# Hybrid chunk-causal layer: weights around the per-layer-input weights requested four tiles ahead, the first two up units' sums on VectorE, the second norm's rows two products later

## The chip, the cores and the metric

One core of one Trainium2 chip runs the whole layer. The metric is the device time of one execution in microseconds; the kernel before was run three times (median 2042.41, from 2042.25 to 2044.58), and once more with the hardware profiler on.

## What is computed

The reference is one layer for two groups of requests: 1024 rows of a prompt and 32 rows of a sample step, 1056 rows of 1024 numbers in all, in float32. Cut to what the change touches:

```python
mix = jax.nn.sigmoid(ga) * (ya @ w_br_a) + jax.nn.sigmoid(gb) * (yb @ w_br_b)
x = x + _rms_norm(mix @ w_out, g_post_mix)
hf = _rms_norm(x, g_pre_ffn)
a, u = jnp.split(hf @ w_up, 2, axis=-1)
...
ffn = (jax.nn.gelu(ac, approximate=True) * u) @ w_down
x = x + _rms_norm(ffn, g_post_ffn)
x = x + (pe @ w_ple) * jax.nn.sigmoid(x @ w_ple_gate)
```

Here `ac` is the causal convolution of `a` over three rows, `pe` the per-layer input (256 numbers a row), `w_up` is 1024 by 5632, `w_out` 1024 by 1024, `w_ple` 256 by 1024.

## The kernel before

**Products.** Everything is kept transposed: 128 features on the partitions, rows along the free dimension. A float32 operand is split into a high and a low part (`hi` is the rounded copy, `lo = x - hi`), and a product is three products of TensorE: high by high, high by low, low by high (lines 193 to 195 in `product`, 1536 to 1538 in the up stage). ScalarE makes the high part and VectorE the low one.

**Weights.** `load_raw` asks SyncE's queue for a raw tile of 512 KB (tag `wr`, two buffers). `load_next` makes its two parts (tag `wb`, eight buffers, so four weights at a time): the high part in line 174 on ScalarE, the low part in line 177 on VectorE; the raw buffer is free again after the low part. `next_w(ahead=2)` goes on with `load_next` until the weight asked for and `ahead` more are there. The list `plan` gives the order of the weights. At the place of the change it holds `w_out` columns 0 to 4, then the two tiles of `w_ple`, then `w_out` columns 5 to 7. Below, c0 to c7 are those eight column blocks of `w_out`, and ple0 and ple1 the two tiles of `w_ple`. The parts of ple0 and ple1 stay in their `wb` buffers until the last `ple_product`.

**The stretch that the change touches.** `w_out` is applied twice: first for rows 0 to 527 (`p` = 0, groups 0 and 1 of 264 rows), then for rows 528 to 1055 (`p` = 1, groups 2 and 3). A block is 24 products for each of the two groups. Beside the second pass, the first half is normed and prepared: `pair_norm` sums squares over the features with TensorE (`sums88`, line 1271, one-column products), takes the inverse root on VectorE (`rsqrt`, lines 204 to 210, twelve small instructions in a chain) and spreads it over the partitions with TensorE (`norm_rows`, line 294), from where ScalarE copies it to `rbT` (line 296). `x1_part` forms the new x (VectorE, lines 1294 and 1295), stores it by GpSimd's queue and scales it (ScalarE, line 1298); `x1_squares` squares it; `build_ops` makes the seven right operands of a Strassen-Winograd scheme (`op`, casts in line 1325, low parts in line 1326, sums and differences in lines 1329 to 1337). After c7 come `pair_norm(1, 0.25 / D)`, four `ple_product` (groups 0 to 3, each of eight blocks of six products, copied by ScalarE in line 1360 and stored by GpSimd's queue) and, between them, `x1_part(2)`, `x1_part(3)` and `build_ops(1)`.

**Up units.** Then 22 up units follow, each 128 columns of both halves of `w_up`. `unit_raw` loads the two raw tiles (even units in the `wr` buffers), `unit_parts` makes seven left operands: four sums (lines 1389 to 1391 and 1396, on GpSimd before) and seven pairs of parts (`wt`, lines 1383 and 1384). `up_unit` runs seven steps; in a step, `mults` makes 12 products for each half `p`, into one of three PSUM tiles X, Y, Z, and `after` moves the result on. Unit 0 does the two halves one after the other, and in a different order for the second half (`early`). `last_ops` squares x of rows 528 to 1055 (line 1509) and sums the squares (24 one-column products for each group, the sums of groups 2 and 3) beside unit 0's first half; the norm that they give, `pair_norm(1, 1.0 / D, x1_t[0])`, is called in unit 0's second half. Its result `rbT` is needed by `after(2)` (line 1551), which scales X into `ab`.

**What sets the order.** The program text gives each instruction its priority; a scheduler then orders each engine's instructions by priority and by the times that it expects, and gives out buffers. Each engine runs its own list strictly in that order, and an instruction that waits holds up all behind it. Each DMA queue is in order too.

Of the kernel before, what the change touches and what calls it, by code (L numbers as in the profile page):

```python
# [14 lines left out]
ALU = mybir.AluOpType  # L15
# [3 lines left out]
D = 1024  # L19
# [11 lines left out]
H = 264  # L31
# [3 lines left out]
T88 = ((0, 88), (88, 88), (176, 88))  # L35
# [24 lines left out]
def layer_kernel(  # L60
# [17 lines left out]
    def nm(s):  # L78
        n_names[0] += 1
        return f"{s}_{n_names[0]}"  # L80
# [5 lines left out]
    V, S, G, E = nc.vector, nc.scalar, nc.gpsimd, nc.tensor  # L86
# [95 lines left out]
    def next_w(ahead=2):  # L182
        while len(ready) < min(limit[0], used[0] + 1 + ahead):
            load_next()
        used[0] += 1
        return ready[used[0] - 1]
# [44 lines left out]
    def tr_bank():  # L231
        return bank(pp, "tr", 2)
# [56 lines left out]
    def norm_rows(rs, tiles, out):  # L289

        n = sum(m_ for _, m_ in tiles)
        t = tr_bank()
        for i, (c, m_) in enumerate(tiles):
            E.matmul(t[:, c:c + m_], rs[:m_, i:i + 1].to_broadcast([m_, P]), ident[:m_, :m_],  # L294
                     start=True, stop=True)
        S.copy(out, t[:, :n])
# [7 lines left out]
    with right("ap") as ap:  # L304
# [198 lines left out]
        with tc.tile_pool(name="np", bufs=1, side="right", reuse_waits="tile") as np_:  # L503
# [103 lines left out]
            xt, rs, rb = ([], [], []), [], []  # L607
            for n in range(6):
# [3 lines left out]
                if n == 2:  # L612
                    rows = vector_rows()
# [73 lines left out]
    for j in range(4):  # L687
# [3 lines left out]
        for k in (0, 2):  # L691
# [3 lines left out]
                            op=ALU.subtract)  # L695
# [84 lines left out]
    with right("bp") as bp:  # L780
# [329 lines left out]
        for c in range(4, 8):  # L1110
            u = unit(gate_out(tb_d[c]))
# [27 lines left out]
    with right("mp") as mp:  # L1139
# [30 lines left out]
        for c in range(8):  # L1170
            w = next_w()
# [30 lines left out]
        for c in range(8):  # L1202
            if c % 2:
                p_cols(c // 2)
            w = next_w()
# [32 lines left out]
    rbT = fo.tile([P, T], F32, name="rbT")  # L1238
# [34 lines left out]
    def pair_norm(p, scale, t=None):  # L1273

        sums = t is None
        t = t or tr_bank()
        v = fo.tile([P, 6], F32, tag="nv", name=nm("nv"), bufs=2)
        rs = fo.tile([P, 6], F32, tag="nr", name=nm("nr"), bufs=2)
        V.memset(v[:], 1.0)
        for g in (2 * p, 2 * p + 1) if sums else ():  # L1280
            sums88(t, g, [sqz[g]])
        V.tensor_scalar(v[:88], t[:88, 0:6], scale, EPS, op0=ALU.mult, op1=ALU.add)
        rsqrt(fo, rs[:], v[:], 6)
        for h in range(2):
            o = H * (2 * p + h)
            norm_rows(rs[:, 3 * h:3 * h + 3], T88, rbT[:, o:o + H])

    def x1_part(g):

# [85 lines left out]
    def unit_parts(u):  # L1375

        f1, f2 = raw_w.pop(u)
        s1 = wp.tile([P, 4, P], F32, tag="wb", name=nm("sa"), bufs=8)[:]
        a11, a12, a21, a22 = f1[:, 0:4, :], f1[:, 4:8, :], f2[:, 0:4, :], f2[:, 4:8, :]

        def parts(src):
            t = wp.tile([P, 2, 4, P], F32R, tag="wb", name=nm("wt"), bufs=8)
            S.copy(t[:, 0], src)  # L1383
            V.tensor_tensor(t[:, 1], src, t[:, 0].bitcast(F32), op=ALU.subtract)  # L1384
            ready_w.append(t)


        parts(a11)
        G.tensor_tensor(s1, a21, a22, op=ALU.add)
        G.tensor_tensor(a21, a11, a21, op=ALU.add)  # L1390
        G.tensor_tensor(a11, a11, s1, op=ALU.add)
        yield
        parts(a11)
        yield
        parts(a12)
        G.tensor_tensor(a12, a12, a11, op=ALU.add)
        yield
        parts(a21)
        yield
        parts(s1)  # L1400
        yield
        parts(a22)
        yield
        parts(a12)
        yield
# [19 lines left out]
    for p in range(2):  # L1425
        for c in range(8):
            if p and c == 5:
                ple_w.extend((next_w(), next_w()))
            w = next_w()
            if p and c == 7:  # L1430
                unit_raw(0)
            for g in (2 * p, 2 * p + 1):
                z_out(c, g, block(w, ALL, Ra[g], Rb[g], KS, H))
            if p == 0:
                continue
            if c == 0:
                pair_norm(0, 0.25 / D)
                x1_part(0)
            if c == 1:
                x1_squares(0)  # L1440
                x_load(1)
                x1_part(1)
                op0 = build_ops(0)
            if 2 <= c < 6:
                next(op0)
            if c == 4:
                x1_squares(1)
                p_load(0)
                p_load(1)
            if c == 5:  # L1450
                pair_norm(0, 1.0 / D)
            if c == 6:
                for _ in op0:
                    pass
                x_load(2)
                x_load(3)
# [60 lines left out]
    x1_t = []  # L1517

    def up_unit(u):
        X, Y, Z = (pf.tile([P, 2, 512], F32, tag="st", name=nm("st"), bufs=3) for _ in range(3))  # L1520
        ab = fp.tile([P, 4 + T], F32, tag="ab", name=nm("ab"), bufs=2)
        G.memset(ab[:, 0:2], 0.0)  # L1522
        us = us0 if u == 0 else Up[:, u % 2, :].bitcast(F32)
        us4 = us.rearrange("p (a h c) -> p a h c", a=2, h=2)
        w = {}

        def mults(i, t, first, ps):
            n = 7 * u + i
            if i not in w:
                w[i] = ready_w[n]  # L1530
            for p in ps:
                for k in range(4):
                    wh, wl = w[i][:, 0, k, :], w[i][:, 1, k, :]
                    xh, xl = ops[p][i][:, 0, k, :], ops[p][i][:, 1, k, :]
                    o = t[:, p, 0:H]
                    E.matmul(o, wh, xh, start=first and k == 0, stop=False, skip_group_check=True)  # L1536
                    E.matmul(o, wh, xl, start=False, stop=False, skip_group_check=True)  # L1537
                    E.matmul(o, wl, xh, start=False, stop=k == 3, skip_group_check=True)  # L1538

        def v(t, ps):  # L1540
            return t[:, ps[0]:ps[-1] + 1, 0:H]

        def after(i, ps):
            x, y, zz = v(X, ps), v(Y, ps), v(Z, ps)
            sl = slice(ps[0], ps[-1] + 1)
            if i == 0:
                S.copy(s1c[:, sl], x)
            elif i == 1:
                V.tensor_tensor(U2[:, sl], s1c[:, sl], y, op=ALU.subtract)
            elif i == 2:  # L1550
                V.tensor_tensor(ab[:, 2:2 + T].rearrange("p (a h c) -> p a h c", a=2, h=2)[:, sl, 0, :],
                                x, rb4[:, sl, 0, :], op=ALU.mult)
            elif i == 3:
                V.tensor_tensor(nU3[:, sl], y, s1c[:, sl], op=ALU.subtract)  # L1554
            elif i == 4:
                V.tensor_tensor(us4[:, sl, 1, :], nU3[:, sl], zz, op=ALU.subtract)
            elif i == 5:
                V.tensor_tensor(us4[:, sl, 0, :], y, s1c[:, sl], op=ALU.subtract)
            elif i == 7:

                S.copy(t12[:, sl], zz)
            elif i == 8:
                V.tensor_tensor(nU3[:, sl], nU3[:, sl], t12[:, sl], op=ALU.add)
            else:
                V.tensor_tensor(t12[:, sl], U2[:, sl], zz, op=ALU.add)  # L1565

        def done():

            V.tensor_tensor(ab[:, 2:2 + T].rearrange("p (a h c) -> p a h c", a=2, h=2)[:, :, 1, 0:232],
                            t12[:, :, 0:232], rb4[:, :, 1, 0:232], op=ALU.mult)  # L1570
            for p, o in ((0, 2 + 496), (1, 2 + 1026)):
                V.tensor_tensor(ab[:, o:o + 32], t12[:, p, 232:H], rb4[:, p, 1, 232:H], op=ALU.mult)
            ff_tail(u, ab, us)


        order = ((0, X, True, (0,)), (1, Y, True, (1,)), (2, X, False, (2,)), (3, Y, False, (3,)),
                 (4, Z, True, (4,)), (5, Y, False, (5,)), (6, Z, False, (6,)))
        early = ((0, X, True, (0,)), (6, Z, True, (7,)), (2, X, False, (2,)), (1, Y, True, (1,)),
                 (3, Y, False, (3, 8)), (4, Z, False, (4, 6)), (5, Y, False, (5,)))
        for ps, steps in (((0,), order), ((1,), early)) if u == 0 else (((0, 1), order),):  # L1580
            for n, (i, t, first, then) in enumerate(steps):
                if u:
                    prepare(7 * u + n + AHEAD)
                elif ps == (0,):
                    prepare(min(n + AHEAD, 6))
                else:
                    prepare(n + AHEAD)
                mults(i, t, first, ps)
                if u == 0 and ps == (0,):
                    last_ops(n)  # L1590
                if ps == (1,) and n == 1:
                    pair_norm(1, 1.0 / D, x1_t[0])
                for a in then:
                    after(a, ps)
        done()
# [88 lines left out]
    for g in range(3):  # L1684
        for q in range(2):
            bs = [mm_bank() for _ in range(4)]
            for k in range(0, NF, 2):
                i = k // 6
                hi, lo = chunk[i]
                w = next_w()  # L1690
# [103 lines left out]
```

## Time and profile before

| | us |
|---|---|
| time, median of three runs | 2042.41 |
| time of the profiled execution | 2051.53 |
| its span, first to last instruction | 2049.8 |
| TensorE busy | 2003.4 |
| VectorE busy | 1441.8 |
| ScalarE busy | 959.8 |
| GpSimd busy | 210.8 |

The mean granted TensorE clock is 0.991 of full speed. The views used below are the page, the waits of one engine (who waited for whom), the timeline of one engine (start, duration, engine, line, operation, and in brackets the idle time before it with what ended it), and the windows (busy time of each engine in a stretch, its granted clock, the share of the DMA engines). A matmul in the timeline lasts longer than the distance to the next one, since matmuls are pipelined; the distance between starts is what one costs.

### The profile page before, as it was taken

What the parts mean: (1) busy time and instruction counts of PE and PEld (TensorE: products, weight loads), DVE (VectorE), ACT (ScalarE), POOL (GpSimd) and SP (SyncE); (2) the same over time, 40 slices, a digit from 0 to 9 for tenths busy, and PEclk for the clock granted to TensorE, in tenths of its full rate; (3) what the DMA queues carried; (4) which work ended last, traced back from release to release, by engine and by line L of the source; (5) the groups of instructions that cost most, each with busy time, mean ns of one, the idle gap of its engine ahead of it and who ended that gap; (6) DMA issues with size and microseconds to landing.
All of it is one profiled execution on the core that took longest, in us unless ns stands there. A gap on an engine that the chain in (4) does not pass through costs nothing. (4 is left out here: it accounts for less than half of the span.)

```text
span 2049.8 us, 37423 instructions
## 1 busy us (share of the span) xinstructions
PE 2003.4 (98%) x14366; PEld 1971.3 (96%) x14366; DVE 1441.8 (70%) x3182; ACT 959.8 (47%) x2174; POOL 210.8 (10%) x283
## 2 busy tenths in 40 slices
PE   7999999999999999999999799999999999999998
PEld 6899999999999999999999799999999999999998
DVE  6997788688888888452553777888888883745552
ACT  5555566556666666341224653333333343543432
POOL 2110000000000000000000123232323210000000
PEclk9999999999999999999999899999999999999999
DMA  8422211411111111486653551222222245655543
GB/s 249 132 94 76 77 58 52 153 42 57 57 56 40 52 45 50 149 248 186 180 176 104 157 190 52 77 80 81 77 85 72 89 134 193 213 177 174 168 128 81
DMA packets 250697, 233.79 MB, mean 114 GB/s; under 512 B 12998, under 2 KB 222425, under 8 KB 250518
## 3 DMA queue, kind: packets, MB, share of 16 engines
q1 hardware_dynamic: 245173, 213.55, 33.9%
q0 software_dynamic: 5344, 17.85, 2.5%
q8 instruction: 113, 1.85, 0.4%
q14 instruction: 67, 0.54, 0.1%
HBM read 171.79 MB, written 59.55 MB: 113 GB/s over the span
## 5 line engine op out<-in xcount | busy, mean ns | idle before, releaser
L1536 PE MATMUL st<-op,wt 128*128 128x264 f32 x1232 | 349.3, 284 | 2.8 <-DVE Sp L1554 1.6
L1538 PE MATMUL st<-op,wt 128*128 128x264 f32 x1232 | 350.1, 284 | 0.0
L1537 PE MATMUL st<-op,wt 128*128 128x264 f32 x1232 | 348.5, 283 | 0.0
L177 DVE TENSOR_TENSOR wl<-wr,wh 128x1024 fp32r<-128x1024 f32 x134 | 163.9, 1223 | 145.0 <-ACT wh L174 132.9
L1536 PEld LDWEIGHTS st<-op,wt 128*128 128x128 f32 x1232 | 231.9, 188 | 4.0 <-DVE Sp L1554 2.1
L1537 PEld LDWEIGHTS st<-op,wt 128*128 128x128 f32 x1232 | 232.1, 188 | 0.0
L1538 PEld LDWEIGHTS st<-op,wt 128*128 128x128 f32 x1232 | 231.5, 188 | 0.0
L174 ACT CAST wh<-wr 128x1024 fp32r<-128x1024 f32 x115 | 120.7, 1049 | 204.1 <-PE mm L194 153.2
L1383 ACT CAST wt<-wu 128x512 fp32r<-128x512 f32 x132 | 81.7, 620 | 200.5 <-POOL ab L1522 99.6
L193 PE MATMUL mm<-ac,wh 128*128 128x352 f32 x528 | 171.3, 324 | 2.1 <-DVE Sp L1565 2.1
L195 PE MATMUL mm<-ac,wl 128*128 128x352 f32 x528 | 170.7, 323 | 0.0
L194 PE MATMUL mm<-ac,wh 128*128 128x352 f32 x528 | 170.2, 322 | 0.0
L193 PE MATMUL mm<-La,wh 128*128 128x384 f32 (+1 forms) x504 | 166.9, 332 | 0.0
L194 PE MATMUL mm<-Lb,wh 128*128 128x384 f32 (+1 forms) x504 | 162.7, 323 | 0.0
L195 PE MATMUL mm<-La,wl 128*128 128x384 f32 (+1 forms) x504 | 162.5, 322 | 0.0
L193 PE MATMUL mm<-Ra,wh 128*128 128x264 f32 x512 | 147.4, 288 | 10.3 <-ACT wh L174 9.9
L195 PE MATMUL mm<-Ra,wl 128*128 128x264 f32 x512 | 146.2, 286 | 0.4 <-DVE wl L177 0.4
L194 PE MATMUL mm<-Rb,wh 128*128 128x264 f32 x512 | 146.5, 286 | 0.0
L1384 DVE TENSOR_TENSOR wt<-wu,wt 128x512 fp32r<-128x512 f32 x132 | 108.0, 818 | 44.7 <-ACT wt L1383 44.5
L434 ACT ACTIVATE sc<-sc,st 128x257 f32<-128x257 f32 (+1 forms) x144 | 69.6, 484 | 87.7 <-DVE st L429 81.6
L193 PEld LDWEIGHTS mm<-Ra,wh 128*128 128x128 f32 x512 | 97.9, 191 | 10.9 <-ACT wh L174 10.3
L193 PEld LDWEIGHTS mm<-ac,wh 128*128 128x128 f32 x528 | 99.7, 189 | 2.4 <-DVE Sp L1565 2.4
(454 smaller groups left out, 5730.1 us busy)
## 6 DMA issues: line engine op xcount, KB each, us to landing
wr<-in_w_down_dram SPq DMA_DIRECT2D x66, 512.0 KB
wu<-in_w_up_dram SPq DMA_DIRECT2D x44, 512.0 KB
wu<-in_w_in_dram SPq DMA_DIRECT2D x32, 512.0 KB
wr<-in_w_in_dram SPq DMA_DIRECT2D x26, 512.0 KB
ac<-act_d SPq DMA_DIRECT2D x66, 176.0 KB
act_d<-Up SPq DMA_DIRECT2D x21, 528.0 KB
wr<-in_w_out_dram SPq DMA_DIRECT2D x16, 512.0 KB
ya_d<-ya SPq DMA_DIRECT2D x8, 528.0 KB
```

The costliest lines, as they stand in the source:

```text
L174: S.copy(hi[:], raw[:])
L177: V.tensor_tensor(lo[:], raw[:], hi[:].bitcast(F32), op=ALU.subtract)
L193: E.matmul(ps, wh, a, start=first and n == 0, stop=False)
L194: E.matmul(ps, wh, b, start=False, stop=False)
L195: E.matmul(ps, wl, a, start=False, stop=last and n == len(ks) - 1)
L434: S.activation(sc[:m_, h, b0:e_ + 1], sc[:m_, h, b0:e_ + 1], AF.Exp, bias=st[:m_, 0, h:h + 1], scale=-1.0, accum_out=st[:m_, 1, h:h + 1])
L1383: S.copy(t[:, 0], src)
L1384: V.tensor_tensor(t[:, 1], src, t[:, 0].bitcast(F32), op=ALU.subtract)
L1536: E.matmul(o, wh, xh, start=first and k == 0, stop=False, skip_group_check=True)
L1537: E.matmul(o, wh, xl, start=False, stop=False, skip_group_check=True)
L1538: E.matmul(o, wl, xh, start=False, stop=k == 3, skip_group_check=True)
```

## The change

Four edits.

1. `next_w` is called with `ahead` 4 in place of 2 at c3 and c4 of the second pass.
2. The sums of up units 0 and 1 (eight instructions of 128 by 512) are VectorE's, in place of GpSimd's.
3. `pair_norm` gives back its last step, the `norm_rows` of both groups, as a function where the sums were made before; in unit 0's second half the inverse root is called after step 0 (before: after step 1, with the rows), the rows after step 3.
4. In `early`, `after(2)`, which reads those rows, goes from step 2 to step 4.

```diff
         V.tensor_scalar(v[:88], t[:88, 0:6], scale, EPS, op0=ALU.mult, op1=ALU.add)
         rsqrt(fo, rs[:], v[:], 6)
-        for h in range(2):
-            o = H * (2 * p + h)
-            norm_rows(rs[:, 3 * h:3 * h + 3], T88, rbT[:, o:o + H])
+
+        def rows():
+            for h in range(2):
+                o = H * (2 * p + h)
+                norm_rows(rs[:, 3 * h:3 * h + 3], T88, rbT[:, o:o + H])
+        if sums:
+            rows()
+        return rows
...
+        adder = V if u < 2 else G
         parts(a11)
-        G.tensor_tensor(s1, a21, a22, op=ALU.add)
-        G.tensor_tensor(a21, a11, a21, op=ALU.add)
-        G.tensor_tensor(a11, a11, s1, op=ALU.add)
+        adder.tensor_tensor(s1, a21, a22, op=ALU.add)
+        adder.tensor_tensor(a21, a11, a21, op=ALU.add)
+        adder.tensor_tensor(a11, a11, s1, op=ALU.add)
...
-        G.tensor_tensor(a12, a12, a11, op=ALU.add)
+        adder.tensor_tensor(a12, a12, a11, op=ALU.add)
...
-            w = next_w()
+            w = next_w(4 if p and c in (3, 4) else 2)
...
-        early = ((0, X, True, (0,)), (6, Z, True, (7,)), (2, X, False, (2,)), (1, Y, True, (1,)),
-                 (3, Y, False, (3, 8)), (4, Z, False, (4, 6)), (5, Y, False, (5,)))
+        early = ((0, X, True, (0,)), (6, Z, True, (7,)), (2, X, False, ()), (1, Y, True, (1,)),
+                 (3, Y, False, (3, 8, 2)), (4, Z, False, (4, 6)), (5, Y, False, (5,)))
...
-                if ps == (1,) and n == 1:
-                    pair_norm(1, 1.0 / D, x1_t[0])
+                if ps == (1,) and n == 0:
+                    x1_t.append(pair_norm(1, 1.0 / D, x1_t[0]))
+                if ps == (1,) and n == 3:
+                    x1_t[1]()
```

**The order on ScalarE, c3 to c5.** Before, from the copies out of c3's second group (`mm_14180`) on; `wr_14216` is ple1's raw tile and `wr_14299` c5's.

```order
L174 CAST wh_14218<-wr_14216 128x1024
L1245 ACTIVATE z_13354<-mm_14180,gph 128x264
L1250 ACTIVATE sq_14206<-mm_14180 128x264
L1325 CAST op_14280<-z_13351 128x1056
L1298 ACTIVATE z_13352<-x_2285_14060,gvec 128x264 x4
...
L1325 CAST op_14284<-z_13352 128x1056
L1304 ACTIVATE x_2285_14060<-x_2285_14060 128x1056
L1325 CAST op_14213<-z_13352 128x1056
L174 CAST wh_14301<-wr_14299 128x1024
L1325 CAST op_14375<-z_13351 128x1056
L1325 CAST op_14470<-z_13351 128x1056
L174 CAST wh_14307<-wr_14305 128x1024
```

In the changed kernel `wr_14151` is ple1's raw tile, `wr_14157` c5's and `wr_14228` c6's; `mm_14163` and `mm_14192` are c3's two groups.

```order
L174 CAST wh_14153<-wr_14151 128x1024
L1245 ACTIVATE z_13353<-mm_14163,gph 128x264
L174 CAST wh_14159<-wr_14157 128x1024
L1250 ACTIVATE sq_14189<-mm_14163 128x264
L1245 ACTIVATE z_13354<-mm_14192,gph 128x264
L1250 ACTIVATE sq_14218<-mm_14192 128x264
L1330 CAST op_14292<-z_13351 128x1056
L1303 ACTIVATE z_13352<-x_2285_14060,gvec 128x264 x4
L1245 ACTIVATE z_13353<-mm_14234,gph 128x264
L1330 CAST op_14221<-z_13352 128x1056
L174 CAST wh_14230<-wr_14228 128x1024
```

c5's cast stood behind the copies of c3 and c4, six casts of `op`, the scaling and two squares; now it stands two rows behind ple1's cast, and c6's stands among c4's copies.

**The order on VectorE after the products of c5.** In the changed kernel: `nv`, `rsb`, `rst` and `nr` with 143xx are the inverse root of rows 0 to 527, `wr_14311` is c7's raw tile, `wu_14481` the second raw tile of up unit 0, `sa` its first sum.

```order
L177 TENSOR_TENSOR wl_14314<-wr_14311,wh_14313 128x1024
...
L209 TENSOR_TENSOR rst_14390<-rst_14390,nv_14379 128x6
L1389 TENSOR_TENSOR wt_14542<-wu_14479,wt_14542 128x512
L210 SCALAR_TENSOR_TENSOR nr_14380<-rst_14390,rsb_14389 128x6
L1395 TENSOR_TENSOR sa_14541<-wu_14481 128x512
L208 SCALAR_TENSOR_TENSOR rst_14390<-nr_14380 128x6
L1396 TENSOR_TENSOR wu_14481<-wu_14479,wu_14481 128x512
L209 TENSOR_TENSOR rst_14390<-rst_14390,nv_14379 128x6
L1251 TENSOR_TENSOR sqz_13365<-sqz_13365,sq_14538 128x264
L210 SCALAR_TENSOR_TENSOR nr_14380<-rst_14390,nr_14380 128x6
L1397 TENSOR_TENSOR wu_14479<-wu_14479,sa_14541 128x512
```

Before, the same inverse root ran with only c7's low part and one sum of squares between its instructions, and the sums of the unit were rows of GpSimd's list:

```order
L209 TENSOR_TENSOR rst_14390<-rst_14390,nv_14379 128x6
L177 TENSOR_TENSOR wl_14314<-wr_14311,wh_14313 128x1024
L1251 TENSOR_TENSOR sqz_13365<-sqz_13365,sq_14372 128x264
L210 SCALAR_TENSOR_TENSOR nr_14380<-rst_14390,rsb_14389 128x6
L208 SCALAR_TENSOR_TENSOR rst_14390<-nr_14380 128x6
```

c7's low part moved ahead of the inverse root, and three sums of up unit 0 moved in between its instructions.

**The order on TensorE in unit 0's second half.** `tr_15135` and `tr_15140` are the norm's rows before, `tr_15160` and `tr_15165` in the changed kernel, `st` the PSUM tiles of the products. Before:

```order
L1537 MATMUL st_14922<-op_14833,wt_14840 128x264
L1538 MATMUL st_14922<-op_14833,wt_14840 128x264
L1536 MATMUL st_14922<-op_14833,wt_14840 128x264
L294 MATMUL tr_15135<-ident,nr_15119 128x88 x3
L294 MATMUL tr_15140<-ident,nr_15119 128x88 x3
L1537 MATMUL st_14922<-op_14833,wt_14840 128x264
```

After:

```order
L1542 MATMUL st_14923<-op_14830,wt_14755 128x264
L1543 MATMUL st_14923<-op_14830,wt_14755 128x264
L1544 MATMUL st_14923<-op_14830,wt_14755 128x264
L294 MATMUL tr_15160<-ident,nr_15106 128x88 x3
L294 MATMUL tr_15165<-ident,nr_15106 128x88 x3
L1542 MATMUL st_14924<-op_15021,wt_14947 128x264
```

Before, the rows stood after 7 of the 12 products of the second half's third step; now they stand behind the whole of its fourth step, 17 products further on.

## The prediction

> **What bounds the kernel now.** I read the page first, then TensorE's waits, then the windows of the stretch that the change touches, then the timelines of its engines.
>
> ```profile
> span 2049.8 us, 37423 instructions
> PE 2003.4 (98%) x14366; PEld 1971.3 (96%) x14366; DVE 1441.8 (70%) x3182; ACT 959.8 (47%) x2174; POOL 210.8 (10%) x283
> ```
>
> TensorE is busy for 98%, so only its waits and slow places can be won. Its waits between 1140 and 1262 us:
>
> ```profile
> PE mm L193 <- ACT wh L174: 9.9, 2, 6.5
> PE tr L294 <- DVE nr L210: 4.4, 2, 3.2
> PE st L1536 <- DVE Sp L1554: 1.6, 1, 1.6
> PE st L1536 <- DVE Sp L1549: 0.6, 1, 0.6
> PE mm L195 <- DVE wl L177: 0.4, 1, 0.4
> PE st L1536 <- DVE ab L1551: 0.4, 1, 0.4
> PE tr L294 <- DVE nv L1279: 0.2, 1, 0.2
> ```
>
> The columns are the sum in us, how often, and the longest. All but the 0.6 (in unit 1) lie in the touched stretch: 16.9 us. The windows cut it at the end of c4, near c7's end, at up unit 0 and at up unit 1; the columns used are the length, the busy time of each engine, and PEclk, the granted clock.
>
> ```profile
> 1149.25:1170.00 20.75, 10.42 (x57) 9.81 (x58) 16.45 (x21) 10.76 (x15) 2.99 (x4) 0.67 0.62 180
> 1170.00:1183.30 13.30, 13.12 (x111) 12.94 (x111) 7.57 (x19) 4.78 (x13) 4.28 (x3) 1.00 0.19 59
> 1183.30:1216.10 32.80, 31.57 (x270) 31.39 (x269) 25.56 (x33) 24.06 (x60) 9.53 (x12) 0.95 0.63 213
> 1216.10:1250.20 34.10, 28.78 (x222) 27.85 (x222) 21.68 (x42) 10.18 (x18) 6.91 (x7) 0.90 0.28 81
> ```
>
> The clock is below 1 in three of them. What that costs is in TensorE's timeline:
>
> ```profile
> 1155.70 0.59 PE L193 MATMUL mm<-Ra,wh 128*128 128x264 f32 x1 [6.45 <-ACT wh L174]
> 1160.41 0.59 PE L193 MATMUL mm<-Ra,wh 128*128 128x264 f32 x1 [3.46 <-ACT wh L174]
> 1163.12 0.42 PE L193 MATMUL mm<-Ra,wh 128*128 128x264 f32 x1
> 1163.34 0.42 PE L194 MATMUL mm<-Rb,wh 128*128 128x264 f32 x1
> 1202.33 0.28 PE L194 MATMUL mm<-pc,wh 128*128 128x264 f32 x1
> 1202.45 0.28 PE L195 MATMUL mm<-pc,wl 128*128 128x264 f32 x1
> ```
>
> Start to start a product takes 0.12 us at full clock and 0.22 behind the two waits: 0.10 lost each.
>
> **Edit 1, the weights.** First ScalarE's casts of ple1, c5 and c6, then VectorE's low parts of ple0, ple1, c5 and c6, then SyncE's queue with the loads of c5 to c7 and one window (its last two columns are the DMA share and GB/s).
>
> ```profile
> 1142.83 1.08 ACT L174 CAST wh<-wr 128x1024 fp32r<-128x1024 f32 x1
> 1154.59 1.05 ACT L174 CAST wh<-wr 128x1024 fp32r<-128x1024 f32 x1
> 1159.32 1.04 ACT L174 CAST wh<-wr 128x1024 fp32r<-128x1024 f32 x1
> ```
> ```profile
> 1137.19 1.22 DVE L177 TENSOR_TENSOR wl<-wr,wh 128x1024 fp32r<-128x1024 f32 x1
> 1148.22 1.22 DVE L177 TENSOR_TENSOR wl<-wr,wh 128x1024 fp32r<-128x1024 f32 x1
> 1160.15 1.22 DVE L177 TENSOR_TENSOR wl<-wr,wh 128x1024 fp32r<-128x1024 f32 x1
> 1161.63 1.22 DVE L177 TENSOR_TENSOR wl<-wr,wh 128x1024 fp32r<-128x1024 f32 x1
> ```
> ```profile
> 1138.47 23.29 SPq L164 DMA_DIRECT2D wr<-in_w_out_dram  x3
> 1144.00:1146.00 2.00, 2.00 (x19) 2.00 (x18) 0.47 (x1) 1.54 (x3) 0.00 (x0) 1.00 0.08 30
> ```
>
> c5's raw tile is asked for at 1138.47, when ple0's low part has freed the buffer, and the DMA share is down to 0.08 by 1144 to 1146: c5 has landed by about 1144.7, ten microseconds before its cast. It is held by its place in ScalarE's list, not by the load. In the new order it follows ple1's cast (now two copies earlier, near 1142.2 to 1143.2) and one copy, and waits there for the landing, about 1 us. Behind it are only copies of c3, whose PSUM banks c6 needs first. Done at 1145.8; its low part follows two VectorE instructions later, at about 1149.0, and c4 ends at 1149.25 (1155.70 less 6.45). That is close, but a miss costs tenths. ple1's low part comes 3.5 us earlier too, so c6 loads from about 1144.7 and is cast near 1151, needed at 1155.
>
> So the 9.9 and 0.4 go, and the half clock behind them: from 1161.4 to 1166.9 about 25 products, 2.5 us. What is late next is c7's low part. VectorE does the same work ahead of it as it did ahead of c6's (end 1162.85), plus one low part more (1.14), less one sum (0.35) and less the idle gap that ple1's part fills (1.1): 1162.5. TensorE wants it at 1149.25 + two blocks (2 x 48 x 0.12 = 11.6) + sums and seven products (1.2) = 1162.1. I take 0.7 for this new wait, between 0 and 2. **Edit 1: 9.9 + 0.4 + 2.5 - 0.7 = 12.1.**
>
> **Edit 2, the sums.** Their price on VectorE is that of a low part of the same shape, start to start:
>
> ```profile
> 1219.05 0.68 DVE L1384 TENSOR_TENSOR wt<-wu,wt 128x512 fp32r<-128x512 f32 x1
> 1219.65 0.68 DVE L1384 TENSOR_TENSOR wt<-sa,wt 128x512 fp32r<-128x512 f32 x1
> 1186.75 1.29 POOL L1396 TENSOR_TENSOR wu<-wu 128x512 f32<-128x512 f32 x1 [4.81 <-DVE rsb L204]
> 1186.93 1.13 DVE L208 SCALAR_TENSOR_TENSOR rst<-rsb 128x6 f32<-128x6 f32 x1
> ```
>
> 0.60 us each, 4.8 for eight. On GpSimd one takes 1.29, and a small VectorE instruction beside it took 1.13 where its neighbours take 0.17. The Trainium skill, SBUF — State Buffer, Who interferes with whom, says that a VectorE instruction with two SBUF inputs and a GpSimd one that reads SBUF lock each other out for the whole instruction; the row agrees. By it the edit frees VectorE of up to eight blocks of about 1 us, by the row alone of one here.
>
> Three sums now stand inside the inverse root for rows 0 to 527, with two casts' low parts around. That root ends at about 1172, and its rows stand on TensorE some 23 products after c7, at 1169 + 3 = 1172: a new wait of 0.6, between 0 and 2.5. The root for `pair_norm(1, 0.25 / D)` loses its 1.13, and one sum (0.60) takes its place: of the 1.2 us that its rows waited (4.4 less 3.2), 0.4 stay. **Edit 2 there: +0.8 - 0.6 = 0.2.** GpSimd's queue had the sums ahead of the stores of `ple`, which waited for ScalarE anyway (as the last one, below): nothing.
>
> **Edits 3 and 4, the rows.**
>
> ```profile
> 1239.69 2.83 PE L294 MATMUL tr<-ident,nr 88*128 88x88 f32 x12 [3.17 <-DVE nr L210]
> 1173.78 1.54 PE L294 MATMUL tr<-ident,nr 88*128 88x88 f32 x12 [0.18 <-DVE nv L1279]
> 1232.91 0.16 DVE L1282 TENSOR_SCALAR nv<-tr 88x6 f32<-88x6 f32 x1 [1.85 <-PE tr L1271]
> 1239.37 0.17 DVE L210 SCALAR_TENSOR_TENSOR nr<-rst,nr 128x6 f32<-128x6 f32 x1
> ```
>
> The wait of 3.2 stands here, and the half clock behind it: the rows take 2.83 where 1.54 is usual (1.3), and 14 products follow at 0.22 (1.4). The root took 6.6 us. The rows now stand 17 products later (2.0 us), the root's start goes up by two instructions, and three sums (1.8) replace stalls of about the same size. I leave 0.5 of the wait, between 0 and 3: too short for the half clock. **3.2 + 2.7 - 0.5 = 5.4.** `after(2)` goes with them; its X is read in time, since X is next written in unit 1.
>
> **What stays.** The 1.6 and 0.4 before unit 0's step 5 come from here:
>
> ```profile
> 1217.93 0.76 POOL L1362 DMA_DIRECT2D ple_d<-ple  x1 [3.68 <-ACT op L1325]
> 1224.00 0.43 DVE L1551 TENSOR_TENSOR ab<-st,rbT 128x264 f32<-128x264 f32 x1 [2.72 <-DMA ple_d<-ple]
> ```
>
> The last `ple` store must land before `ab` may be written in its place; that distance is untouched. The one-column sums also cost clock, without a wait:
>
> ```profile
> 1202.94 3.85 PE L1271 MATMUL tr<-ones,x 128*88 128x1 f32 x48
> 1208.23 0.42 PE L195 MATMUL mm<-pc,wl 128*128 128x264 f32 x1
> ```
>
> After 24 of them (two records each) 15 products ran at 0.22: 1.5 us. Now both groups come as 4 and 20 (3.2 us). I count that one of the two bursts halves the clock: 0, with 1.5 either way. The Trainium skill, TensorE: Matmul & The Clock Gate, Part 1: The HAM clock gate, says that a window of about 3.4 us idle halves the clock. The waits agree (6.45 and 3.46 did, 1.6 did not; 3.17 did, a little under); the burst, with TensorE never idle, does not fit it. By the rule alone no burst costs anything, and the sum would be 1.5 more.
>
> **The sum.** 12.1 + 0.2 + 5.4 = 17.7, and 0.3 for half of the small waits behind roots and sums: 18.0. The profiled execution took 2051.53 (span 2049.8), 9.1 over the median of the three runs; scaled by 2042.41/2051.53 it would be 17.9. I take 18.0 from the median: 2024.4. The floor: 16.9 of waits and 6.7 of half clock (2.5, 2.7, 1.5) are all there is, 23.6.
>
> **Rivals.**
> - *VectorE becomes the bound.* It is busy 16.45 of 20.75 us in the first window and gets 4.8 more. If the two roots and the later half of `build_ops` each come 3 us late, TensorE waits 3 times 3 us, and two such waits halve the clock (2.7 each): 18.0 - 14.4 = 3.6, 2038.8. With half of that 2031.6. For: the list runs in order. Against: VectorE idles 5.7 us in the second window and over 7 in the third.
> - *c5 still late.* If the cast holds for a load that lands near 1149 instead of 1144.7, c5 waits 4 us and the clock falls: 18.0 - 6.7 = 11.3, 2031.1. The 0.08 speaks against it. It is also the way in which the edit would not do what it says.
> - *Both bursts halve the clock, and a wait passes 3 us:* -4.2, 2028.6. By the quoted rule neither burst does, 2022.9.
> - *Slower.* The first sum waits on VectorE for unit 0's second raw tile, which is asked for only after c7's low part (about 1163), and both roots are behind it. Up to about 1169 that costs nothing; each us more moves the rows, and with them x1 and unit 0. To end 4.1 us slower it would have to land 22 us late. Against it: c5's raw tile, of the same size, landed within 6.3 us of 1138.47.
>
> **Chances.** The forecast with 1.5 either way and its faster variants 0.62; both bursts 0.14; VectorE in half size 0.12 and in full 0.04; c5 late 0.05; slower 0.02; 0.01 left for no change. Low end: the floor from the lowest run, 2042.25 - 23.6 = 2018.6, less 1.1 for half the spread of the three runs. High end: VectorE in half size, 2031.5. About 0.2% (4.1 us) is what a measurement of this kernel can tell from no change. Full-size VectorE (2038.8) lies at its edge: faster 0.94, same 0.04, slower 0.02.
>
> **What would show it.** Right: no wait for `wh` in line 193 around c5 to c7, PEclk 1.00 there, c7 ending near 1169; a wait of under 1 us for c7's `wl`; the rows of the norms waiting under 1 us; unit 1 starting near 1232. Wrong: c5's cast on ScalarE behind a wait for the DMA past 1149, VectorE without a gap from 1160 to 1200, or unit 1 starting after 1240.

## The result, and the profile after

| | before | after |
|---|---|---|
| median of four runs each, on one chip | 2042.59 (2042.25 to 2044.58) | 2030.9 (2027.15 to 2033.31) |
| ratio | | 0.9939 [0.9922, 0.9956] |
| again, in a later set (nine runs and five) | 2044.9 (2042.04 to 2050.28) | 2033.18 (2024.42 to 2034.8) |
| ratio | | 0.9939 [0.9925, 0.9953] |
| profiled executions | 2051.53, 2049.48 | 2031.59, 2024.42 |

After is 12.5 us faster (0.0061 x 2045; 9.6 to 15.3 by the later set). The forecast was 18.0, its time 2024.4 in a range up to 2031.5. So sign and range held, 2030.9 close to the range's end, and a third of the gain is missing. The later set asked whether the three runs of before had hidden some of it: 0.992 was expected if so, and the ratio stayed.

The page of the first execution, and TensorE's waits from 1131 to 1262 us (sum, how often, longest):

```profile
span 2029.7 us, 37418 instructions
PE 1994.4 (98%) x14366; PEld 1964.1 (97%) x14366; DVE 1438.5 (71%) x3190; ACT 959.1 (47%) x2174; POOL 200.0 (10%) x275
```
```profile
PE tr L1271 <- DVE x L1515: 2.1, 1, 2.1
PE st L1542 <- DVE Sp L1560: 0.9, 1, 0.9
PE mm L195 <- DVE wl L177: 0.7, 1, 0.7
```

The waits for `wh` (9.9), for the norm rows (4.4) and the 1.6 and 0.4 before step 5 are gone. c7's low part makes TensorE wait 0.7, as forecast. New is the 2.1: the first one-column sums wait for the squares of x (line 1515). On VectorE these stand behind the new x and a low part, without a gap of over 0.21 us since 1177.53, and that last gap is for the store of the x that they overwrite:

```profile
1177.53 2.43 DVE L1299 TENSOR_TENSOR z<-z,rbT 128x1056 f32<-128x1056 f32 x2 [1.47 <-ACT rbT L296]
...
1188.35 1.26 DVE L1515 TENSOR_TENSOR x<-x 128x1056 f32<-128x1056 f32 x1 [0.21 <-DMA x_d<-x]
```

The 0.9 lies in unit 1.

The windows, cut near the end of c4, at the norm's rows behind c7, at the first burst of one-column sums (up unit 0 follows) and at the second norm's rows; first this execution, then the second one of the same kernel (length, busy time of PE, PEld, DVE, ACT, POOL, the granted clock, DMA share, GB/s):

```profile
1146.00:1170.00 24.00, 23.27 (x196) 23.06 (x195) 23.90 (x43) 17.39 (x33) 3.75 (x5) 1.00 0.58 174
1170.00:1199.30 29.30, 27.07 (x217) 26.71 (x217) 25.44 (x36) 22.74 (x56) 8.28 (x11) 0.94 0.71 249
1199.30:1226.90 27.60, 27.60 (x222) 27.60 (x221) 15.97 (x36) 7.67 (x15) 0.96 (x3) 0.81 0.37 107
```
```profile
1145.00:1169.00 24.00, 23.22 (x196) 23.02 (x194) 23.56 (x45) 17.60 (x34) 3.08 (x5) 1.00 0.56 172
1169.00:1196.50 27.50, 24.91 (x211) 24.55 (x210) 23.93 (x33) 21.29 (x54) 8.26 (x11) 1.00 0.72 248
1196.50:1220.80 24.30, 23.39 (x222) 23.15 (x221) 16.92 (x38) 8.24 (x15) 0.96 (x3) 1.00 0.45 131
```

c5 to c7 run at clock 1.00 in both, where before had 0.67. Unit 0 with the same work (222 matmul records) takes 27.6 us at 0.81 in one execution and 24.3 at 1.00 in the other. TensorE's timeline of the first shows where; a product takes 0.12 us start to start at full clock, 0.22 at half (durations 0.28 and 0.42):

```profile
1189.76 0.76 PE L1271 MATMUL tr<-ones,x 128*88 128x1 f32 x8 [2.10 <-DVE x L1515]
...
1192.03 0.42 PE L193 MATMUL mm<-pc,wh 128*128 128x264 f32 x1
1192.25 0.42 PE L194 MATMUL mm<-pc,wh 128*128 128x264 f32 x1
...
1199.30 3.58 PE L1271 MATMUL tr<-ones,x 128*88 128x1 f32 x40
1202.74 0.57 PE L1542 MATMUL st<-op,wt 128*128 128x264 f32 x1
1203.11 0.42 PE L1543 MATMUL st<-op,wt 128*128 128x264 f32 x1
1203.33 0.42 PE L1544 MATMUL st<-op,wt 128*128 128x264 f32 x1
...
1215.06 3.22 PE L1271 MATMUL tr<-ones,x 128*88 128x1 f32 x40
...
1219.31 0.42 PE L1543 MATMUL st<-op,wt 128*128 128x264 f32 x1
1219.53 0.42 PE L1544 MATMUL st<-op,wt 128*128 128x264 f32 x1
```

Three phases of 14, 26 and 14 products ran at half clock: one behind the new wait and four sums, one behind each burst of 20 sums (two records each). 54 x 0.10 = 5.4 us. The second execution has the same waits (2.5 in place of 2.1, and 0.9 is left before step 5) and bursts, and no half-clock phase at all:

```profile
1188.48 0.76 PE L1271 MATMUL tr<-ones,x 128*88 128x1 f32 x8 [2.47 <-DVE x L1515]
1196.50 3.23 PE L1271 MATMUL tr<-ones,x 128*88 128x1 f32 x40
...
1210.38 3.28 PE L1271 MATMUL tr<-ones,x 128*88 128x1 f32 x40
```
```profile
1200.04 0.28 PE L1542 MATMUL st<-op,wt 128*128 128x264 f32 x1
1200.16 0.28 PE L1543 MATMUL st<-op,wt 128*128 128x264 f32 x1
```

To compare kernels, I use **the stretch**: from the start of the first norm's rows (line 294, near 1127 us, ahead of all edits) to the start of the first copy of up unit 1 out of X (ScalarE's `Sp<-st`; it is the fourth such row of a trace, two copies of X and one of Z by unit 0 come first). Both starts are rows of each trace. In before it lasted 126.1 and 125.5 us, in after 109.1 and 104.8. Behind it, to the end, before took 796.4 and 792.4, after 794.0 and 792.9: after loses nothing there.

### The profile page after: what moved, and what is told of

The parts are those of the page before. It is cut to its first block, busy times and chain, and to the rows that moved or that the text cites. A ratio compares the mean times of both kernels' runs of the same rounds, so it can differ in the third digit from the quotient of the medians.

```text
span 2029.7 us, 37418 instructions
## 1 busy us (share of the span) xinstructions
PE 1994.4 (98%) x14366; PEld 1964.1 (97%) x14366; DVE 1438.5 (71%) x3190; ACT 959.1 (47%) x2174; POOL 200.0 (10%) x275
## 4 chain that ended last, share of the span: by engine, by line
PE 79%; DMA 7%; DVE 6%; issue 3%; ACT 3%; SPq 1%; POOL 0%; ACTq 0%; DVEq 0%; POOLq 0%
PE mm L193 11%; PE mm L195 11%; PE mm L194 11%; PE st L1544 7%; PE st L1542 7%; PE st L1543 7%; PE G L811 2%; PE G L808 2%; PE G L810 2%; PE Y L808 1%; PE Y L811 1%; PE Y L810 1%; PE tr L450 1%; DMA ld<-yb_d 1%; DMA mx_d<-ta 1%
## 5 line engine op out<-in xcount | busy, mean ns | idle before, releaser
L193 PEld LDWEIGHTS mm<-ac,wh 128*128 128x128 f32 x528 | 99.0, 187 | 2.0 <-DVE Sp L1571 2.0
L194 PEld LDWEIGHTS mm<-ac,wh 128*128 128x128 f32 x528 | 99.6, 189 | 0.0
```

Source lines behind the costliest of these rows:

```text
L193: E.matmul(ps, wh, a, start=first and n == 0, stop=False)
L194: E.matmul(ps, wh, b, start=False, stop=False)
```

## The experiments

Gains below are (1 - ratio) x 2045, with the ratio's interval. The question: the profiled pair was 20 us apart, the timed runs 12. Which edit brings what, and what is the rest?

| kernel | ratio to before | gain, us | stretch, us |
|---|---|---|---|
| before again | 1.0005 [0.9991, 1.0019] | -1.0 [-3.9, 1.8] | 125.5 |
| edit 1 alone | 0.9982 [0.9968, 0.9996] | 3.7 [0.8, 6.5] | 120.8 |
| edit 2 alone | 0.9974 [0.9961, 0.9986] | 5.3 [2.9, 8.0] | 118.7 |
| edits 3, 4 alone | 0.9994 [0.9982, 1.0005] | 1.2 [-1.0, 3.7] | 122.3 |
| edits 1, 2 | 0.9919 [0.9897, 0.9940] | 16.6 [12.3, 21.1] | 110.9 |
| edits 1, 3, 4 | 0.9967 [0.9955, 0.9980] | 6.7 [4.1, 9.2] | 116.2 |
| edits 2, 3, 4 | 0.9968 [0.9952, 0.9984] | 6.5 [3.3, 9.8] | 120.0 |
| after (all) | 0.9939 [0.9925, 0.9953] | 12.5 [9.6, 15.3] | 109.1, 104.8 |
| after, half the sums | 0.9884 [0.9870, 0.9897] | 23.7 [21.1, 26.6] | 101.7 |
| the same, again | 0.9898 [0.9879, 0.9917] | 20.9 [17.0, 24.7] | 101.6 |
| after, few sums | 0.9896 [0.9882, 0.9909] | 21.3 [18.6, 24.1] | 101.2 |
| before, half the sums | 0.9997 [0.9983, 1.0011] | 0.6 [-2.2, 3.5] | 126.5 |

**Before again**, unchanged.

> The kernel before, run and profiled again. Its first profiled execution took 2051.5 us, 9 over its timed runs, and the trace of after shows the same work up to 1140 us within 0.7 us of it; so the 9 us should lie behind 1140 us. Theory A: the wait for c5 to c7's casts (9.9) and the half clock behind it (2.5) are there in every execution, and the 9 us lie elsewhere: then this trace has 9 to 10 us of waits in line 193 on wh and unit 1 still starts near 1250. Rival B: that stall was long only in the execution of the first profile: then an execution of about 2042 to 2045 us shows a wait for wh of 2 to 5 us with less half clock, and unit 1 starts near 1242, and edit 1 is worth about 6 us and not 12.

This execution took 2049.5 us with the same waits: 10.4 for `wh` in the whole kernel, 9.3 of it at c5 and c6, 3.2 for the second norm's rows, and the half clock behind both. Unit 1's first copy came at 1255.3. Rival B falls: the stall is not peculiar to one execution. But before's runs spread from 2038.3 to 2054.6 (66 runs beside those of other kernels, medians 2045.98, 2044.9 and 2045.95), so that the three runs shown before the prediction, with a median of 2042.41, were low by about 3 us. (After's four runs of that set were low too: the ratio is the same in both sets.) Of the 9 us by which the first profiled execution was longer than its timed runs, 4.0 lie behind the stretch. Part of that spread lies ahead of all edits: over the fourteen traces of this study the first norm's rows start between 1123.2 and 1131.1 us. The windows from 25 to 50 us, of edit 2 alone (rows at 1123.2) and of edits 1 and 2 (1131.1), differ in the granted clock, which is not all of it (after's first execution, at 1.00 as well, has the rows at 1126.6):

```profile
25.00:50.00 25.00, 24.10 (x139) 20.67 (x137) 20.85 (x62) 14.29 (x33) 4.64 (x10) 1.00 0.85 227
```
```profile
25.00:50.00 25.00, 22.65 (x108) 18.66 (x107) 15.55 (x42) 12.51 (x27) 4.66 (x10) 0.80 0.68 214
```

**Edit 1 alone.**

```diff
-            w = next_w()
+            w = next_w(4 if p and c in (3, 4) else 2)
```

> Edit 1 alone (the weights asked for ahead at c3 and c4). By the forecast it is worth 12.1 us: 2030.4. By rival B (the stall is shorter in the timed runs than in the profiled one) 4 to 7 us: 2035.5 to 2038.5. In both the wait for wh at c5 to c7 is gone and about 0.7 us of wait for c7's low part stands in its place.

The wait for `wh` is gone, 0.8 for c7's low part stands there, and yet only 3.7 us were gained. TensorE's timeline shows a new wait behind c7, and VectorE's and GpSimd's timelines show its cause:

```profile
1171.33 2.83 PE L294 MATMUL tr<-ident,nr 88*128 88x88 f32 x12 [3.74 <-DVE nr L210]
```
```profile
1165.81 1.25 DVE L210 SCALAR_TENSOR_TENSOR nr<-rst,rsb 128x6 f32<-128x6 f32 x1
1167.10 0.17 DVE L208 SCALAR_TENSOR_TENSOR rst<-nr 128x6 f32<-128x6 f32 x1
1167.30 1.12 DVE L209 TENSOR_TENSOR rst<-rst,nv 128x6 f32<-128x6 f32 x1
1168.45 0.17 DVE L210 SCALAR_TENSOR_TENSOR nr<-rst,nr 128x6 f32<-128x6 f32 x1
1168.65 1.15 DVE L208 SCALAR_TENSOR_TENSOR rst<-nr 128x6 f32<-128x6 f32 x1
1169.84 0.17 DVE L209 TENSOR_TENSOR rst<-rst,nv 128x6 f32<-128x6 f32 x1
1170.04 1.15 DVE L210 SCALAR_TENSOR_TENSOR nr<-rst,nr 128x6 f32<-128x6 f32 x1
```
```profile
1165.60 1.44 POOL L1389 TENSOR_TENSOR sa<-wu 128x512 f32<-128x512 f32 x1 [6.06 <-DMA wu<-in_w_up_dram]
1167.12 1.27 POOL L1390 TENSOR_TENSOR wu<-wu,wu 128x512 f32<-128x512 f32 x1
1168.34 1.52 POOL L1260 DMA_DIRECT2D x<-xt_d  x2
1169.88 1.27 POOL L1391 TENSOR_TENSOR wu<-wu,sa 128x512 f32<-128x512 f32 x1
```

With c5 to c7 earlier, GpSimd's work (three sums, one issue of two loads) falls on the inverse root; in before, the issue stood ahead of the root (1165.80) and the sums behind it (from 1177.50). Four of the root's small instructions take 1.12 to 1.25 where their neighbours take 0.17: 4.0 us more in all, each of them beside one of those four GpSimd entries. The root is late, TensorE waits 3.74, and half clock follows. The Trainium skill, SBUF — State Buffer, Who interferes with whom, says that a VectorE instruction with two SBUF inputs contends with a GpSimd instruction that reads SBUF; beside the three sums this trace agrees with it, 1.12 to 1.25 beside 0.17. Beside the issue of loads one instruction took 1.15 as well, and the one before it (1168.45), beside the same issue, 0.17.

**Edit 2 alone, and after without it.** In the second kernel `adder = V if u < 2 else G` becomes `adder = G`.

> Edit 2 alone (the eight sums of up units 0 and 1 on VectorE). Forecast: 0.2 us gained, 2042.3, with the small waits behind sums and roots (0.3) gone at best. If the lock between VectorE and GpSimd had cost VectorE up to 1 us for each of the eight sums, up to 3 us: 2039.5. If VectorE is the bound, 2 to 4 us slower: 2045.

> After with the eight sums back on GpSimd. By the forecast's step (edit 2 is worth 0.2) the time is that of after. By the rival, which the run of edit 1 alone suggests (there the root behind c7 was late by 3.7 us and the clock halved behind it), edit 1's gain needs edit 2: 6 to 9 us slower than after, with a wait of about 3.7 us for the norm's rows behind c7 and PEclk under 0.9 there.

Edit 2 alone gained 5.3, far over the 0.2 forecast; taking it out of after costs 5.8 (12.5 less 6.7), a little under the 6 to 9 of the rival. Without it the rows behind c7 wait 3.74 again:

```profile
1172.22 2.83 PE L294 MATMUL tr<-ident,nr 88*128 88x88 f32 x12 [3.74 <-DVE nr L210]
```

In after, the same root stands among VectorE's own sums, and none of its instructions is stretched:

```profile
1167.19 0.69 DVE L1395 TENSOR_TENSOR sa<-wu 128x512 f32<-128x512 f32 x1
1167.80 0.16 DVE L208 SCALAR_TENSOR_TENSOR rst<-nr 128x6 f32<-128x6 f32 x1
1167.91 0.69 DVE L1396 TENSOR_TENSOR wu<-wu,wu 128x512 f32<-128x512 f32 x1
1168.52 0.16 DVE L209 TENSOR_TENSOR rst<-rst,nv 128x6 f32<-128x6 f32 x1
```

At the second norm, the root of before has three stretched instructions beside GpSimd's sums; with edit 2 alone that root has none of over 0.17:

```profile
1235.19 1.25 DVE L210 SCALAR_TENSOR_TENSOR nr<-rst,rsb 128x6 f32<-128x6 f32 x1
1236.68 1.11 DVE L209 TENSOR_TENSOR rst<-rst,nv 128x6 f32<-128x6 f32 x1
1238.03 1.11 DVE L208 SCALAR_TENSOR_TENSOR rst<-nr 128x6 f32<-128x6 f32 x1
```

Edit 2 also changed TensorE's order there. In before 29 products stand between group 3's last sum and the rows, with edit 2 alone 41, and the rows' wait of 3.2 fell to nothing without edits 3 and 4.

**Edits 3 and 4 alone, and after without them.**

> Edits 3 and 4 alone (the root one step earlier, the rows two steps later, after(2) with them). Forecast: 5.4 us gained, 2037.1: the wait for the norm (3.2) and the half clock behind it (2.7) go. If another half-clock phase behind the one-column sums stays or takes its place, 3 to 4 us: 2039.

> After without edits 3 and 4 (edits 1 and 2 alone). Forecast: 5.4 us slower than after, with a wait of over 3 us for the second norm's rows. Theory E: edit 2 has already moved the sums of group 3 up on TensorE (3.22 us in one burst behind step 5 instead of 10 and 30 records later), so that the rows wait about 1 us or less without edits 3 and 4: 0 to 2 us slower than after, and their worth of 5.4 was really edit 2's.

Alone, edits 3 and 4 put 46 products between group 3's last sum and the rows, 17 more than before, as the prediction read from the order (two steps of the unit, which the title calls two products). The wait fell by 2.0 us, to 1.2 where 0.5 was forecast, and the rows went at full clock:

```profile
1239.75 1.54 PE L294 MATMUL tr<-ident,nr 88*128 88x88 f32 x12 [1.19 <-DVE nr L210]
1241.55 0.39 PE L1542 MATMUL st<-op,wt 128*128 128x264 f32 x1 [0.26 <-DVE Sp L1555]
```

But 14 products behind them still ran at half clock. The stretch of this trace is 3.2 to 3.8 us shorter, as in the second expectation; the gain of the timed runs, 1.2, can't be told from none. With edits 1 and 2 there are 54 products and no wait for the rows, with all four 59. So edits 3 and 4 took away a wait that edit 2 had taken already. Edits 1 and 2 without them measured 16.6, all four 12.5; the intervals overlap, and I draw only that 3 and 4 add nothing that these runs can show. That execution has the new wait for the squares as 3.2 (2.1 and 2.5 in after):

```profile
1195.39 0.76 PE L1271 MATMUL tr<-ones,x 128*88 128x1 f32 x8 [3.18 <-DVE x L1511]
```

**After without edit 1.**

> After without edit 1 (edits 2, 3 and 4 alone). By the forecast edit 1 is worth 12.1 us: 2044 to 2045, the time of before less little. By what the profiles of edit 2 alone (stretch 7 us shorter) and of after (17 and 21 us shorter) show, the waits for wh (10 us) and the half clock behind them (1.5 to 2.5) stay: 8 to 12 us slower than after, and 2 to 6 faster than before.

6.5 us faster than before, a little over the 2 to 6 expected from the profiles, and 6 slower than after, under the 8 to 12: the waits of 6.0 and 3.5 for `wh` are back. Edit 1 with the others in place is worth 6 by the timed runs (12.5 less 6.5), and 10.9 to 15.3 by the stretch of the profiles. Edits 1 and 2 alone add up to 9.0, together they gain 16.6 (12.5 with 3 and 4). So edit 1 needs edit 2, without which the wait behind c7 takes the place of those for `wh`. The reverse isn't shown: edit 2 brings as much alone (5.3) as on top of the other three (5.8).

**Half the sums, few sums.** Both kernels are after with the squares added on VectorE first: in pairs (12 one-column sums for a group instead of 24), or all eight (3).

```diff
                 V.tensor_tensor(x, x, x, op=ALU.mult)
+                V.tensor_tensor(x[:, 0:2, :], x[:, 0:2, :], x[:, 2:4, :], op=ALU.add)
...
-            sums88(x1_t[0], g, [x1q[g][k // 4][:, k % 4, :] for k in range(KT)])
+            sums88(x1_t[0], g, [x1q[g][k // 2][:, k % 2, :] for k in range(4)])
```

> After, with the eight squares of each column of x added in pairs on VectorE (four more instructions of 128 by 528), so that a group takes 12 one-column sums on TensorE and not 24. Theory C (a burst of one-column sums of over 3 us halves the clock): the bursts are now of 10 (1.6 us), no half-clock phase stands behind them, and 4 to 6 us of half clock and 3 us of sums go, less up to 2.4 for VectorE's additions: 2023 to 2028 beside 2031 for after. Rival D (the half clock comes from the 2.1 us wait and from other places): the phases stay, and only the 3 us of sums go: 2028 to 2031.

> The same, with all eight squares added on VectorE, so that a group takes 3 one-column sums. Theory C: as with half the sums, and 3 us of sums more go, less up to 4.8 for the additions on VectorE, if its chain (squares, additions, root) is what the rows wait for: 2020 to 2027. Rival D: the half clock stays, 2026 to 2031. If VectorE is the bound here, the rows of the second norm wait over 2 us and it is no faster than half the sums.

> After with half the sums, run again. Theory C: no half clock behind its bursts (1.66 us) in this execution either, and executions that spread less than those of after (2024.4 to 2034.8): 2019 to 2023 in all rounds. If a wait of 2.5 us behind ple halves the clock in this execution (it did with few sums, and not with half the sums), one phase of 13 products, 1.4 us, stands there. Rival D: half-clock phases behind the bursts, and a spread of 8 us or more.

Half the sums: 2021.0 (2019.8 to 2022.6) and, in a later set, 2026.1 (2022.2 to 2028.9); 20.9 to 23.7 us faster than before, and so some 8 to 11 faster than after. In its two traces the bursts last 1.66 and no product of the stretch ran at half clock. The second trace had clock 0.80 from 25 to 50 us, and its first norm's rows came 5.3 us later, about the difference of the two spans (2018.6, 2023.7); so the 2019 to 2023 expected of the repeat didn't hold, in the profiled execution for a reason ahead of the edits. This is what theory C forecast, with a size above its better end. The stretch is 3.1 us shorter than in the execution of after without half clock, which is what the two bursts lost themselves (3.2 and 3.3 to 1.7 each); the rest of the gain is then half clock that after has in most executions, which fits, but is inferred. Few sums brought nothing more. In all three traces ScalarE's copy of `ple` makes TensorE wait 2.51; it halved the clock (13 products) in the execution with few sums and not in the two with half the sums (first few sums, then half the sums):

```profile
1190.25 0.59 PE L193 MATMUL mm<-pc,wh 128*128 128x264 f32 x1 [2.51 <-ACT ple L1365]
```
```profile
1187.77 0.39 PE L193 MATMUL mm<-pc,wh 128*128 128x264 f32 x1 [2.51 <-ACT ple L1365]
1202.78 1.66 PE L1271 MATMUL tr<-ones,x 128*88 128x1 f32 x20
1210.93 1.66 PE L1271 MATMUL tr<-ones,x 128*88 128x1 f32 x20
```

**Before with half the sums.**

> Before, with the eight squares added in pairs on VectorE and 12 one-column sums for a group in place of 24, and nothing else. The bursts shrink from 24 and 15 sums (3.85 and 2.44 us) to 12 or 10 (1.6 to 1.9). Theory C (bursts of over 3 us halve the clock): the phase of 14 products at half clock behind the first burst goes (1.4 us), with 3 us of sums: 4 to 5 us faster than before, less up to 2.4 for the additions; the waits of 3.2 us for the second norm and 9.7 for wh stay, with the half clock behind them. If the sums cost nothing but their own time, 1 to 3 us faster.

A miss: no gain (0.6). In the profile VectorE's additions make other things late (the first burst waits 0.7 for the squares, the second norm's rows 3.4 instead of 3.2, `ab` 1.8 instead of 0.4), the phase behind the first burst stayed, with 14 products at half clock, and one of 13 came behind the waits of 1.8 and 1.6 before step 5:

```profile
1200.53 2.25 PE L1271 MATMUL tr<-ones,x 128*88 128x1 f32 x24 [0.69 <-DVE x L1510]
...
1239.25 2.83 PE L294 MATMUL tr<-ident,nr 88*128 88x88 f32 x12 [3.40 <-DVE nr L210]
```

So a shorter burst is no gain by itself: together with the wait ahead of it, the time without a large product was still 3.0 us.

## Why the prediction was right, and where it was not

- **c5 to c7: right.** No wait for `wh`, clock 1.00, 0.7 for c7's low part, as forecast. c5's low part came at 1146.8, two us ahead of the forecast. The price of the edit, 12.1, is within what the profiles show beside the other edits (10.9 to 15.3), and twice the 6 of the timed runs; alone it brought 3.7.
- **The waits in all: right.** The forecast takes 12.8 of 16.9 us of waits away (9.9 + 0.4 - 0.7 + 0.2 + 2.7 + 0.3). Up to unit 1, the two profiles of after still show 2.8 and 4.2: 14.1 and 12.7 gone. But they are other waits than forecast: those before step 5, which the text counts as untouched, went in one execution and shrank to 0.9 in the other, and that for the squares came. This last one is the rival "VectorE becomes the bound" in a small form, in a place that the text doesn't name: from the arrival of the norm's rows to the squares VectorE works without a gap, and the wait is 0.6 with edit 2 but not edit 1, and 2.1 to 3.2 with both.
- **The clock: the term that was mis-sized.** The text has 2.5 and 2.7 of half clock going and 1.5 of one burst staying. Measured: 5.4 stays in one execution, none in the other, where before had 6.7: 1.3 or 6.7 gained, for 5.2 forecast. "One of the two bursts" was a mean over a thing that happens by execution; the rival "both bursts" (2028.6) was the first execution.
- **Edit 2, "0.2": wrong, it was mis-sized.** One stretched instruction was counted where a row showed one. The root at 1233 to 1239 in before's trace has three (1.25, 1.11, 1.11; 3.0 more than three of 0.17), which the text, under edits 3 and 4, sets against three sums "of about the same size" (1.8). With edit 1 the root behind c7 would have had four. The rule of the Trainium skill that the text puts beside the sum, with "up to eight blocks of about 1 us", was nearer. The forecast charged 0.6 for a wait behind that root; no such wait came, as the sums there replaced 4.0 of stalls.
- **Edits 3 and 4, "5.4": wrong as a price of these edits.** 17 products and 2 us, as read from the order; but edit 2 moved the sums up, which wasn't counted, and did the same work; and the half clock stayed in the run of these edits alone. That the sum still came within a third is in part luck: edit 2 was priced some 5 us too low and edits 3 and 4 some 5 too high, and the two errors cancel.
- **The sum and its base.** In the stretch the profiled pair gained 17.0 and, with the second execution of after, 21.4, about the forecast. The timed runs gained 12.5. The second profile of after (2024.4) is the fastest of its nine runs, whose median is 2031.6; between its two profiles 4.4 of 7.1 us lie in the stretch. The mean granted clock of each timed run is on record: 1.000 in the fastest of the nine, 0.997 in the next two (2027.2 and 2028.5), 0.993 to 0.996 in the other six (2030.2 to 2034.8). So the slower executions had a lower clock; that they lost it in this stretch is likely but not shown, since timed runs leave no trace. The start-up, which also varies, doesn't tell the kernels apart, but both widen the measurement: the 0.2% that the text gave as what can be told from no change was too fine for three runs.
- **The slower case** (the sum waits for the second raw tile) didn't come: that sum starts at 1167.2 and the root isn't late.

## What to carry to other kernels

Two edits that look separate can hang together: without the second, the weights came earlier only to put the next step on top of GpSimd's sums, and the price of an edit is what it is worth with the others in place. Count as empty for TensorE's clock not only waits but one-column sums and small transposes beside them; stretches near 3 us are best shortened well below that, or they cost in some executions and not in others. And take several executions of the kernel before as the base where a change is worth half a per cent: its spread is part of the forecast.

## What the runs showed that was not expected

I took from the timelines of the fourteen traces every stretch from about 1130 to 1247 us of over 1.4 us in which TensorE ran no product of 264 columns (the time from 0.12 us after the start of one to the start of the next: waits, one-column sums and transposes of 88 together), and looked whether products behind it ran at half clock:

| without a large product, us | stretches | half clock behind |
|---|---|---|
| 1.5 to 2.3 | 36 | 2 |
| 2.7 to 3.25 | 18 | 9 |
| 3.4 to 8.2 | 28 | 27 |

The two in the first row stand 2 us apart in one trace, the one exception in the last is 3.7, and six of the 28 began at half clock already (the wait of 3.46 in the prediction is one of them). The stretches aren't independent: the same place of the program returns in several kernels. A phase lasts some 12 to 26 products, unless the next wait comes first. TensorE counts as busy through many of these stretches in the profile, so its busy share doesn't show them. The Trainium skill, TensorE: Matmul & The Clock Gate, Part 1: The HAM clock gate, says that the window of about 3.4 us is free-running and that the cost varies from run to run. The traces agree that it varies: in after, stretches of 2.9, 3.4 and 3.2 us halved the clock in one execution, and of 3.25, 3.1 and 3.2 did not in the other. The length they put lower: half of the stretches of 2.7 to 3.25 us halved it. And a stretch needs no wait for it: 24 one-column sums in a row (3.7 us in before) did the same.
